# Where the scales of the down tiles, the sums of the next pair and the last group's scale are issued in an encoder block

## The chip, the cores and the metric

The kernel runs on one core of one Trainium2 chip. The metric is the device time of one execution in microseconds (us), the median of the runs. TensorE (PE) does the matmuls, VectorE (DVE) and ScalarE (ACT) work on tiles in SBUF and PSUM, and loads are issued on the queues of SyncE (SP) and GpSimd (POOL).

## The reference

One layer of a hybrid encoder block on 512 positions of width 2048, in float32. It ends with a gated feed-forward part, which is all that the change touches:

```python
h2 = rms_norm(x, g_ffn[l])
up = causal_dwconv(h2 @ w_up[l], conv_w[l], conv_b[l])   # w_up 2048 x 11264, width-3 taps
a, gate = jnp.split(up, 2, axis=-1)
x = x + (a * jax.nn.silu(gate)) @ w_down[l]              # w_down 5632 x 2048
```

## The kernel before

Weights come from HBM as float32 tiles of 128x1024. So that TensorE can run at its f16 rate, each tile is scaled by a factor that suits its largest row sum and split into two f16 halves, high and low, in one tile `whl` (`split16`, L886: ACT writes the high half on L889, DVE the low half on L890). A product then takes three f16 matmuls for each block: high by high, high by low, low by high (`mm3`, L130).

**Units.** The hidden width is cut into 44 pairs of column blocks (a column block of `a` and the matching one of `gate`). The first four pairs are done by `lead`. Each pair j from 4 to 43 is a unit (`up_unit`, L988): it multiplies a 2x2 block matrix by Strassen's scheme (Winograd's form), so it takes seven products instead of eight, T4, B11, T1, T2, B21, B22, T3, in this order, of 24 matmuls each. Their seven weight tiles are made from four loads and sums of them: `s1` (two tiles added by an accumulating POOL DMA), `a22`, `a11`, `a12`, then `s2` and `s4` (DVE adds in place, L948 and L952), and `s3` (again two tiles added by a DMA). After the seventh product DVE combines the PSUM banks into `z`, the taps follow (L827 to L829), and `gated` (L835) makes the hidden tile `m` of the pair on DVE (L838) and its row sums on ACT (L841).

**Down tiles.** Behind each unit from the fifth pair on, two down tiles are multiplied (`down`, L1059): 24 matmuls each of 512 columns into two PSUM tiles named `mx`, which DVE adds to the accumulators (L1078). The last ten down tiles follow the last unit. Four pairs make a group; a group's hidden tiles are scaled together (`m_scale`) and split (`m_split`, tiles `mhl`) while the first unit of the next group runs, piece by piece from the list `later`.

**Scales.** A scale is one number for all partitions. `abs_sums` (L893) lets ACT sum the absolute values of each row of a tile (tile `junk`, sums in `sm`). `scales` (L763) then takes the row maximum (DVE, L770), puts it on the diagonal of a 128x128 tile (ACT, `dg`, L771), multiplies by ones on TensorE so that each partition sees all 128 maxima (L773, into an `mx` tile), and takes maximum, product and reciprocal on DVE (L774 to L776). `period_scales` does this for a unit and its two down tiles at once: six sums, one multiplication of 256 columns.

**Order.** The program is a list `todo` of steps; a unit has seven steps that make weight tiles, and one for each of its down tiles. Ahead of each product or down tile, `take(3)` runs steps until four weight tiles are ready, so that in the steady state the step run at a product is three places further on. At the seventh product of unit j (T3) that is the first step of unit j+1, `start`, which calls `period_scales`; at the first down tile behind unit j it is the second step of unit j+1. Each engine issues its instructions in one fixed order. That order is not the text's: a planner at build time lets an instruction pass earlier ones that are not ready by its own estimate.

**Pools.** Tiles come from pools by tag. `junk`, `su` (the copy of B11's bank, L997), `mhl` and `m` are all of the tag `act` (48 buffers); the PSUM tiles of L773 and of the down tiles are all of the tag `mx` (4 buffers); raw down tiles have 3 buffers (`raw`), the unit's loads 4 (`ur`), the split tiles 3 under each of two tags.

Of the kernel before, what the change touches and what calls it, by code (L numbers as in the profile page):

```python
# [8 lines left out]
F32 = mybir.dt.float32  # L9
# [4 lines left out]
AF = mybir.ActivationFunctionType  # L14
ALU = mybir.AluOpType
PSUM = bass.MemoryType.PSUM

P = 128
# [5 lines left out]
NPAIR_FF = 44  # L24
N_WARM = 12
NGRP = 11
N_LEAD = 4
H = 256
BND = 16000.0
# [18 lines left out]
C_CW = C_CB + 88  # L48
# [4 lines left out]
def block_kernel(ctx: ExitStack, tc: tile.TileContext, xT, wst, cols, bias_t, masks, yT):  # L53
# [17 lines left out]
    def nm(s):  # L71
        cnt[0] += 1
        return f"{s}{cnt[0]}"
# [10 lines left out]
    def sm_t():  # L84
        return smp.tile([P, 8], F32, tag="sm", name=nm("sm"))
# [4 lines left out]
    def mx_t():  # L90
        return ps_mx.tile([P, T], F32, tag="mx", name=nm("mx"))

    V = nc.vector
    A = nc.scalar
# [3 lines left out]
    def c3(ap, n):  # L98
        return ap.rearrange("p (a b) -> p a b", a=n)
# [36 lines left out]
    colt = cst.tile([P, NC], F32, name="colt")  # L136
# [52 lines left out]
    one = cst.tile([P, 1], F32, name="one")  # L189
# [547 lines left out]
    cwp = ctx.enter_context(tc.tile_pool(name="cwp", bufs=3))  # L737
# [25 lines left out]
    def scales(sets, bound):  # L763


        n = len(sets)
        t = sm_t()
        dg = dgp.tile([P, 2, P], BF16, tag="dg", name=nm("dg"))
        for i, r in enumerate(sets):
            V.tensor_reduce(out=t[:, i:i + 1], in_=r, axis=mybir.AxisListType.X, op=ALU.max)  # L770
            A.activation(dg[:, i], ident, AF.Copy, scale=t[:, i:i + 1])  # L771
        psm = c3(mx_t()[:, 0:2 * P], 2)
        PE.matmul(psm[:, 0:n], lhsT=on1b, rhs=dg[:, 0:n], start=True, stop=True)  # L773
        V.tensor_reduce(out=t[:, 2:2 + n], in_=psm[:, 0:n], axis=mybir.AxisListType.X, op=ALU.max)  # L774
        V.tensor_scalar(out=t[:, 4:4 + n], in0=t[:, 2:2 + n], scalar1=1.01 / bound, scalar2=1e-30, op0=ALU.mult, op1=ALU.add)
        V.reciprocal(out=t[:, 6:6 + n], in_=t[:, 4:4 + n])  # L776
        return [(t[:, 4 + i:5 + i], t[:, 6 + i:7 + i]) for i in range(n)]

    def junk_t():
        return actp.tile([P, 1024], F16, tag="act", name=nm("junk"))  # L780

    gs = cst.tile([P, KT], F32, name="gs")
    inv_h = cst.tile([P, 1], F32, name="inv_h")
# [78 lines left out]
    todo, ready, later = [], [], []  # L862
# [16 lines left out]
    def load_sum(t, i, k):  # L879
        nc.sync.dma_start(out=t, in_=wst[i])  # L880
        nc.gpsimd.dma_start(out=t, in_=wst[k], accum_op=ALU.add)
        return t
# [10 lines left out]
    def abs_sums(r, tiles):  # L893
        for k, t in enumerate(tiles):
            A.activation(junk_t(), t, AF.Abs, accum_out=r[:, k:k + 1])  # L895

    units = {}
    DOWNS = [(g, c2) for g in range(NGRP) for c2 in range(8)]
    N_BESIDE = 2 * (NPAIR_FF - N_LEAD - 1)

    def unit_loads(j):
        u = units.setdefault(j, {})
        i = N_MIX + 16 + 4 * (j - N_LEAD)
        u["s1"] = load_sum(ur_t(), i + 2, i + 3)
        u["a22"] = load(ur_t(), i + 3)
        u["a11"] = load(ur_t(), i)
        u["a12"] = load(spare2 if j % 2 else ur_t(), i + 1)

    def down_loads(ds):
        at_end = DOWNS.index(ds[0]) - N_BESIDE  # L910
        new = ur_t if at_end >= 0 and at_end % 4 == 0 else raw_t
        return [load(new(), N_DOWN + 8 * g + c2) for g, c2 in ds]

    def period_scales(j, ds):

        r = sm_t()
        sets = []
        u = units.get(j)
        if u is not None:
            abs_sums(r[:, 0:4], [u[n] for n in ("s1", "a22", "a11", "a12")])  # L920
            sets.append(r[:, 0:4])
        if ds:
            raws = down_loads(ds)
            abs_sums(r[:, 4:8], raws)
            sets.append(r[:, 4:4 + len(ds)])
        sc = scales(sets, BND)
        dt = [(raw, *sc[-1]) for raw in raws] if ds else []
        if u is not None:
            h = cwp.tile([P, 1], F32, tag="uh", name=nm("uh"))
            V.tensor_tensor(out=h, in0=sc[0][0], in1=inv_h, op=ALU.mult)  # L930
            cw = cwp.tile([P, 2, 3], F32, tag="cw", name=nm("cw"))
            A.activation(cw, c3(colt[:, C_CW:C_CW + 3 * 88], 2)[:, :, 3 * j:3 * j + 3], AF.Copy, scale=h)
            u.update(s=sc[0][1], cw=cw, ds=dt)
        return dt

    def plan_unit(j, ds):
        u = units.setdefault(j, {})

        def whl(n):
            ready.append(split16(u[n], u["s"]))  # L940

        def start():
            if "s" not in u:
                period_scales(j, ds)
            whl("a22")

        def s2():
            V.tensor_tensor(out=u["a11"], in0=u["s1"], in1=u["a11"], op=ALU.add)  # L948
            whl("a11")

        def s4():
            V.tensor_tensor(out=u["a12"], in0=u["a11"], in1=u["a12"], op=ALU.add)  # L952
            whl("a12")
            if j + 1 < NPAIR_FF:
                unit_loads(j + 1)

        def s3():
            i = N_MIX + 16 + 4 * (j - N_LEAD)
            u["s3"] = load_sum(raw_t() if j == N_LEAD else spare, i, i + 2)
            whl("s3")  # L960

        todo.extend([start, lambda: whl("a11"), lambda: whl("s1"), s2, lambda: whl("a12"), s4, s3])
        todo.extend([lambda k=k: down_split(u["ds"][k]) for k in range(len(ds))])

    def down_split(d):
        raw, inv, s = d
        ready.append((split16(raw, s), inv))

    def plan_downs(ds):

        st = []

        def one(k):
            if k == 0:
                st.extend(period_scales(None, ds))
            down_split(st[k])
        todo.extend([lambda k=k: one(k) for k in range(len(ds))])

# [45 lines left out]
    def lead():  # L1024
        half = N_LEAD // 2
        n = 0
        for j in range(half):
            u = c3(ur_t(), 2)
            for e in range(2):
                ps = mm_t()  # L1030
                for h in range(2):
                    wh, wl = next_w()
                    for k in range(8):
                        cs = slice(k * P, (k + 1) * P)
                        kt = 8 * h + k
                        mm3(ps, wh[:, cs], wl[:, cs], hh[kt], hl_[kt], kt == 0, kt == KT - 1)
                        if n == 0 and k == 3:
                            finish_r2()
                    if n in (2, 4, 6):
                        t_prep(n // 2 - 1)  # L1040
                    n += 1
                evict_r2(ps, u[:, e])
            lead_taps(j, [u[:, 0], u[:, 1]], (ssa, rmask)[j])
        unit_loads(N_LEAD)
        pss = [mm_t() for _ in range(2 * half)]
        for i in range(8):
            wh, wl = next_w()
            for e, kt in enumerate((i, i + 8)):
                for c in range(2 * half):
                    cs = slice((4 * e + c) * P, (4 * e + c + 1) * P)  # L1050
                    mm3(pss[c], wh[:, cs], wl[:, cs], hh[kt], hl_[kt], i + e == 0, i + e == 8)
            if i in (1, 2, 4, 6, 7):
                t_prep((0, 3, 4, 0, 5, 0, 6, 7)[i])
            if i == 4:
                period_scales(N_LEAD, [])
        us = [evict_r2(ps, actp.tile([P, T], F32, tag="act", name=nm("u"))) for ps in pss]
        later.extend([lambda j=j: lead_taps(half + j, us[2 * j:2 * j + 2]) for j in range(half)])

# [22 lines left out]

    mrp = ctx.enter_context(tc.tile_pool(name="mrp", bufs=2))
    steps = []
    queue = DOWNS
    done = 0
    for j in range(N_LEAD, NPAIR_FF):
        steps.append(j)
        n = 0 if j == N_LEAD else 2
        ds = queue[done:done + n]
        done += n  # L1090
        plan_unit(j, ds)
        steps += ds
    for k in range(done, len(queue), 2):
        plan_downs(queue[k:k + 2])
    steps += queue[done:]

    gate_taps = colt[:, C_CW + 3 * (NPAIR_FF + N_LEAD):C_CW + 3 * 88]
    A.activation(gate_taps, gate_taps, AF.Copy, scale=-1.0)
# [2 lines left out]
    for st in steps:  # L1101
        if isinstance(st, tuple):
            down(*st)
            continue
        up_unit(st)
        if st == N_LEAD:
            m_scale(0)
            for j in range(4):
                m_split(j)
        elif st % 4 == 3:  # L1110
            g = st // 4
            later.append(lambda g=g: (m_scale(g), m_split(4 * g)))
            later.extend([lambda j=j: m_split(j) for j in range(4 * g + 1, 4 * g + 4)])
        if st == NPAIR_FF - 1:
            while later:
                later.pop(0)()


def _level_masks(np):
# [121 lines left out]
```

## Time and profile before

| | us |
|---|---|
| median of 3 runs | 2279.82 |
| lowest and highest | 2278.26, 2281.75 |
| the profiled execution | 2279.07 |
| its span, first to last instruction | 2277.3 |
| PE busy in the span | 2200.5 (97%) |
| DVE busy | 1672.4 (73%) |
| ACT busy | 1336.8 (59%) |
| DMA queue q1, share of 16 engines | 32.4% |

The profiled execution lies 0.75 us under the median. The feed-forward units run from about 1010 to 2199 us of the span, the last ten down tiles with the two of the last unit from 2199 us to the end. A busy share is an average over the span; what a stage waits for is seen in the waits and the timeline of that stage.

### The profile page before, as it was taken

How to read it: one execution, taken by the hardware profiler on the slowest of the kernel's cores; microseconds unless marked ns; L12 is line 12 of the kernel's file. 1: busy time of each engine (PE TensorE's matmuls, PEld its weight loads, DVE VectorE, ACT ScalarE, POOL GpSimd, SP SyncE). 2: the span in 40 equal slices, each digit the busy share in tenths (PEclk: the TensorE clock that was granted, in tenths of full speed). 3: DMA queues.
4: the chain of work that ended last, by engine and by line, in shares of the span. 5: the costliest groups of instructions: out<-in, count | busy, mean ns of one | idle time of the engine just before them, and what ended most of it. 6: DMA issues, size and time to landing. Idle time of an engine off the chain costs nothing.

```text
span 2277.3 us, 34675 instructions
## 1 busy us (share of the span) xinstructions
PE 2200.5 (97%) x13667; PEld 1694.6 (74%) x13667; DVE 1672.4 (73%) x2729; ACT 1336.8 (59%) x2119; POOL 271.3 (12%) x261
## 2 busy tenths in 40 slices
PE   9999999999999999998999999999999999999989
PEld 7888888788888888785667777776776777777654
DVE  7678658857658744787777777787877777778764
ACT  5455445545445424457676767776667776767661
POOL 5223123310001103100000000000000000000001
PEclk9999999999999999999999999999999999999999
DMA  6222222232222333445555565555555666655532
GB/s 211 88 70 75 84 93 65 77 99 84 86 91 93 125 117 101 129 140 131 166 158 164 161 162 162 158 157 153 148 164 158 167 167 167 158 156 160 149 91 83
DMA packets 82755, 294.21 MB, mean 129 GB/s; under 512 B 9568, under 2 KB 10208, under 8 KB 82592
## 3 DMA queue, kind: packets, MB, share of 16 engines
q1 hardware_dynamic: 68112, 240.34, 32.4%
q0 software_dynamic: 14480, 51.65, 12.0%
q8 instruction: 107, 1.75, 0.3%
q14 instruction: 56, 0.46, 0.1%
HBM read 287.76 MB, written 4.19 MB: 128 GB/s over the span
## 4 chain that ended last, share of the span: by engine, by line
PE 49%; DVE 28%; ACT 11%; issue 6%; DMA 6%; POOL 0%; SPq 0%; ACTq 0%; DVEq 0%; POOLq 0%
PE mm L131 12%; PE mm L133 12%; PE mm L132 12%; DVE whl L890 8%; DMA raw<-wst 5%; ACT junk L895 4%; ACT whl L889 4%; DVE vo L1078 3%; PE mx L133 3%; PE mx L131 3%; PE mx L132 3%; DVE vo L828 2%; DVE vo L829 2%; DVE ur L948 1%; ACT dg L771 1%
## 5 line engine op out<-in xcount | busy, mean ns | idle before, releaser
L131 PE MATMUL mm<-th,whl 128*128 128x256 f16 x2240 | 612.5, 273 | 5.9 <-ACT whl L889 5.9
L133 PE MATMUL mm<-th,whl 128*128 128x256 f16 x2240 | 612.3, 273 | 2.6 <-DVE whl L890 2.6
L132 PE MATMUL mm<-tl,whl 128*128 128x256 f16 x2240 | 612.3, 273 | 0.0
L131 PE MATMUL mm<-act,whi 128*128 128x512 f32 x1024 | 406.4, 397 | 0.0
L133 PE MATMUL mm<-act,wlo 128*128 128x512 f32 x1024 | 399.4, 390 | 0.0
L131 PEld LDWEIGHTS <-whl 128*128 128x128 f16 x2948 | 289.1, 98 | 147.9 <-issue 32.0
L132 PE MATMUL mm<-act,whi 128*128 128x512 f32 x1024 | 398.8, 389 | 0.0
L133 PEld LDWEIGHTS <-whl 128*128 128x128 f16 x2948 | 289.2, 98 | 133.7 <-issue 22.5
L132 PEld LDWEIGHTS <-whl 128*128 128x128 f16 x2948 | 289.2, 98 | 108.5 <-issue 0.8
L889 ACT ACTIVATE whl<-ur,sm 128x1024 f16<-128x1024 f32 x206 | 231.1, 1142 | 154.2 <-DVE ur L948 52.1
L119 ACT CAST whi<-raw 128x1024 fp32r<-128x1024 f32 (+1 forms) x161 | 167.7, 1042 | 228.9 <-PE mm L132 183.7
L890 DVE SCALAR_TENSOR_TENSOR whl<-ur,sm,whl 128x1024 f16<-128x1024 f32 x206 | 261.4, 1277 | 41.0 <-ACT whl L889 41.0
L122 DVE TENSOR_TENSOR wlo<-raw,whi 128x1024 fp32r<-128x1024 f32 (+1 forms) x161 | 209.5, 1302 | 91.5 <-ACT whi L119 86.7
L131 PE MATMUL mx<-mhl,whl 128*128 128x512 f16 x708 | 268.5, 379 | 0.0
L132 PE MATMUL mx<-mhl,whl 128*128 128x512 f16 x708 | 268.4, 379 | 0.0
L133 PE MATMUL mx<-mhl,whl 128*128 128x512 f16 x708 | 268.2, 379 | 0.0
L133 PEld LDWEIGHTS mm<-act,wlo 128*128 128x128 f32 x1024 | 192.2, 188 | 41.2
L131 PEld LDWEIGHTS mm<-act,whi 128*128 128x128 f32 x1024 | 192.4, 188 | 38.8 <-issue 0.5
L132 PEld LDWEIGHTS mm<-act,whi 128*128 128x128 f32 x1024 | 192.5, 188 | 38.1 <-issue 0.5
L895 ACT ACTIVATE junk<-ur 128x1024 f16<-128x1024 f32 x146 | 152.1, 1044 | 0.0
L1078 DVE SCALAR_TENSOR_TENSOR vo<-mx,inv,vo 128x512 f32<-128x512 f32 x177 | 130.3, 741 | 25.1 <-PE mx L133 25.1
L890 DVE SCALAR_TENSOR_TENSOR whl<-raw,sm,whl 128x1024 f16<-128x1024 f32 x83 | 106.3, 1283 | 43.1 <-ACT whl L889 42.2
(285 smaller groups left out, 3022.7 us busy)
## 6 DMA issues: line engine op xcount, KB each, us to landing
raw<-wst SPq DMA_DIRECT2D x242, 512.0 KB, 3.5
ur<-wst SPq DMA_DIRECT2D x146, 512.0 KB, 3.5
spare<-wst SPq DMA_DIRECT2D x59, 512.0 KB, 4.8
ur<-wst POOLq DMA_DIRECT2D x40, 512.0 KB, 5.6
spare<-wst POOLq DMA_DIRECT2D x39, 512.0 KB, 8.0
vo<-xT SPq DMA_DIRECT2D x16, 256.0 KB, 5.3
vo<-xT POOLq DMA_DIRECT2D x16, 256.0 KB, 3.1
yT<-vo POOLq DMA_DIRECT2D x13, 256.0 KB, 2.3
```

Of the source, the lines that this page charges most:

```text
L119: A.copy(out=hi[:, c], in_=raw[:, c])
L122: V.tensor_tensor(out=lo[:, c], in0=raw[:, c], in1=hi[:, c].bitcast(F32), op=ALU.subtract)
L131: PE.matmul(ps, lhsT=sh, rhs=mh, start=start, stop=False)
L132: PE.matmul(ps, lhsT=sh, rhs=ml, start=False, stop=False)
L133: PE.matmul(ps, lhsT=sl, rhs=mh, start=False, stop=stop)
L771: A.activation(dg[:, i], ident, AF.Copy, scale=t[:, i:i + 1])
L828: V.scalar_tensor_tensor(out=y[:, 1:], in0=u[:, :T - 1], scalar=cw[:, 1:2], in1=y[:, 1:], op0=ALU.mult, op1=ALU.add)
L829: V.scalar_tensor_tensor(out=y[:, 2:], in0=u[:, :T - 2], scalar=cw[:, 0:1], in1=y[:, 2:], op0=ALU.mult, op1=ALU.add)
L889: A.activation(t[:, 0:1024], x, AF.Copy, scale=s)
L890: V.scalar_tensor_tensor(out=t[:, 1024:], in0=x, scalar=s, in1=t[:, 0:1024], op0=ALU.mult, op1=ALU.subtract)
L895: A.activation(junk_t(), t, AF.Abs, accum_out=r[:, k:k + 1])
L1078: V.scalar_tensor_tensor(out=acc[c][:, ts_], in0=ps[:, ts_], scalar=inv, in1=acc[c][:, ts_], op0=ALU.mult, op1=ALU.add)
```

## The change

`period_scales` is split into three functions. `unit_sums` makes the row sums of chosen tiles of a unit, `unit_scale` makes the unit's scale from the four sums, and `down_scale` makes the scale of a pair of down tiles, with an L773 multiplication of its own (128 columns). They are called from other steps:

- the loads of unit j+1 and the sums of its `s1` and `a22` in the step that splits `a12` of unit j; the sums of its `a11` and `a12` in the step of `s4`; its scale in the step of `s3`, so all ahead of the steps that split the down tiles of unit j
- the loads of unit j+1's down tiles in the last step of unit j (the last down split), and their scale in the second step of unit j+1, behind the split of `a11`
- `m_scale` of the last group, with its four splits, was run right behind the last unit; now the scale and the first split come behind two more down tiles, the other three splits behind a third

```diff
-    def period_scales(j, ds):
+    def unit_sums(j, names):
+        u = units[j]
+        if "r" not in u:
+            u["r"] = sm_t()
+        for n in names:
+            k = ("s1", "a22", "a11", "a12").index(n)
+            abs_sums(u["r"][:, k:k + 1], [u[n]])
+
+    def unit_scale(j):
+        u = units[j]
+        (inv, s), = scales([u["r"][:, 0:4]], BND)
...
+    def down_scale(raws):
         r = sm_t()
...
+        abs_sums(r, raws)
+        (inv, s), = scales([r[:, 0:len(raws)]], BND)
+        return [(raw, inv, s) for raw in raws]
...
-        def start():
-            if "s" not in u:
-                period_scales(j, ds)
-            whl("a22")
+        def p1():
+            whl("a11")
+            if ds:
+                u["ds"] = down_scale(u["raws"])
...
+        def p2():
+            whl("a12")
+            if nxt:
+                unit_loads(j + 1)
+                unit_sums(j + 1, ("s1", "a22"))
+
         def s4():
             V.tensor_tensor(out=u["a12"], in0=u["a11"], in1=u["a12"], op=ALU.add)
             whl("a12")
-            if j + 1 < NPAIR_FF:
-                unit_loads(j + 1)
+            if nxt:
+                unit_sums(j + 1, ("a11", "a12"))
...
             whl("s3")
+            if nxt:
+                unit_scale(j + 1)
...
-        todo.extend([start, lambda: whl("a11"), lambda: whl("s1"), s2, lambda: whl("a12"), s4, s3])
-        todo.extend([lambda k=k: down_split(u["ds"][k]) for k in range(len(ds))])
+        todo.extend([lambda: whl("a22"), p1, lambda: whl("s1"), s2, p2, s4, s3])
+        for k in range(max(len(ds), 1)):
+            def one(k=k):
+                if ds:
+                    down_split(u["ds"][k])
+                if k == max(len(ds), 1) - 1 and nxt:
+                    units[j + 1]["raws"] = down_loads(beside(j + 1))
...
     for st in steps:
         if isinstance(st, tuple):
             down(*st)
+            if st in DOWNS[N_BESIDE - 1:N_BESIDE + 1] and later:
+                later.pop(0)()
+                while later and st == DOWNS[N_BESIDE]:
+                    later.pop(0)()
             continue
...
-        if st == NPAIR_FF - 1:
-            while later:
-                later.pop(0)()
```

## Rows read from the trace of the kernel before

**Rows 1.** Span and granted clock of the core.
```profile
core 0: 2277.3 us, clock 0.996
```

**Rows 2.** Waits of PE in the feed-forward units: us in total, times, longest us.
```profile
PE mx L773 <- ACT dg L771: 46.8, 34, 9.7
PE mm L131 <- ACT whl L889: 5.9, 3, 3.3
```

**Rows 3.** Groups by form, 1130 to 2200 us: busy us, mean ns | idle before us.
```profile
L773 PE MATMUL mx<-dg,on1b 128*128 128x256 bf16 x35 | 9.4, 270 | 32.6 <-ACT dg L771 32.6
```

**Rows 4.** Timeline of PE at four L773 multiplications: start, us, [idle before <- releaser].
```profile
1153.23 0.27 PE L773 MATMUL mx<-dg,on1b 128*128 128x256 bf16 x1 [2.02 <-ACT dg L771]
...
1272.94 0.27 PE L773 MATMUL mx<-dg,on1b 128*128 128x256 bf16 x1 [2.02 <-ACT dg L771]
1273.05 0.27 PE L133 MATMUL mm<-th,whl 128*128 128x256 f16 x1
...
1301.59 0.27 PE L773 MATMUL mx<-dg,on1b 128*128 128x256 bf16 x1 [0.55 <-ACT dg L771]
...
2108.28 0.27 PE L773 MATMUL mx<-dg,on1b 128*128 128x256 bf16 x1 [2.01 <-ACT dg L771]
```

**Rows 5.** Timeline of PE behind the last unit's seventh product.
```profile
2198.83 0.27 PE L133 MATMUL mm<-th,whl 128*128 128x256 f16 x1
...
2208.77 0.27 PE L773 MATMUL mx<-dg,on1b 128*128 128x128 bf16 x1 [9.67 <-ACT dg L771]
2208.83 0.63 PE L131 MATMUL mx<-mhl,whl 128*128 128x512 f16 x1
2209.26 0.63 PE L132 MATMUL mx<-mhl,whl 128*128 128x512 f16 x1
```

**Rows 6.** Timeline of PE from a seventh product over two down tiles to the next unit.
```profile
1243.53 0.27 PE L132 MATMUL mm<-tl,whl 128*128 128x256 f16 x1
1243.64 0.27 PE L133 MATMUL mm<-th,whl 128*128 128x256 f16 x1
1243.75 0.38 PE L131 MATMUL mx<-mhl,whl 128*128 128x512 f16 x1
...
1254.11 0.27 PE L131 MATMUL mm<-th,whl 128*128 128x256 f16 x1
```

**Rows 7.** Timeline of ACT in a unit without group splits.
```profile
1230.24 0.35 ACT L997 COPY su<-mm 128x256 f32<-128x256 f32 x1
1230.49 1.15 ACT L889 ACTIVATE whl<-raw,sm 128x1024 f16<-128x1024 f32 x1
...
1239.20 1.06 ACT L895 ACTIVATE junk<-raw 128x1024 f16<-128x1024 f32 x1 [1.32 <-DMA raw<-wst]
```

**Rows 8.** Timeline of ACT in the next unit, which has the group splits.
```profile
1260.58 1.13 ACT L889 ACTIVATE whl<-raw,sm 128x1024 f16<-128x1024 f32 x1
1262.16 1.34 ACT L856 ACTIVATE mhl<-m,mg 128x512 f16<-128x512 f32 x2 [0.45 <-DVE mg L850]
1263.40 0.35 ACT L997 COPY su<-mm 128x256 f32<-128x256 f32 x1
...
1265.93 1.05 ACT L895 ACTIVATE junk<-ur 128x1024 f16<-128x1024 f32 x1
...
1268.01 1.05 ACT L895 ACTIVATE junk<-ur 128x1024 f16<-128x1024 f32 x1
...
1274.17 1.15 ACT L889 ACTIVATE whl<-ur,sm 128x1024 f16<-128x1024 f32 x1 [1.28 <-DVE uh L930]
```

**Rows 9.** Timeline of DVE around the stretch of rows 6, and behind the last unit.
```profile
1243.46 1.28 DVE L890 SCALAR_TENSOR_TENSOR whl<-ur,sm,whl 128x1024 f16<-128x1024 f32 x1 [1.17 <-ACT whl L889]
...
1252.57 0.68 DVE L838 TENSOR_TENSOR m<-vo,vo 128x512 f32<-128x512 f32 x1
1253.17 0.74 DVE L1078 SCALAR_TENSOR_TENSOR vo<-mx,inv,vo 128x512 f32<-128x512 f32 x1
1253.83 1.21 DVE L948 TENSOR_TENSOR ur<-ur,ur 128x1024 f32<-128x1024 f32 x1
...
2206.59 0.69 DVE L838 TENSOR_TENSOR m<-vo,vo 128x512 f32<-128x512 f32 x1 [0.76 <-ACT vo L837]
```

**Rows 10.** Timeline of ACT behind the last unit.
```profile
2207.31 0.63 ACT L841 ACTIVATE z<-m 128x512 f32<-128x512 f32 x1 [0.76 <-DVE m L838]
2207.85 0.19 ACT L841 ACTIVATION_READ_ACCUMULATOR z<-m 128x1 f32 x1
...
2209.98 2.56 ACT L856 ACTIVATE mhl<-m,mg 128x512 f16<-128x512 f32 x4 [1.25 <-DVE mg L850]
```

**Rows 11.** Timeline of the SP queue, loads for the next unit.
```profile
1255.11 4.77 SPq L876 DMA_DIRECT2D ur<-wst  x2
```

**Rows 12.** Stretches: us, busy us (x instructions) of PE, PEld, DVE, ACT, POOL; PE clock; DMA.
```profile
1054.00:1058.00 4.00, 0.68 (x7) 0.37 (x5) 0.10 (x1) 1.28 (x2) 0.00 (x0) 1.00 0.73 267
1059.77:1063.18 3.41, 3.25 (x16) 2.14 (x15) 1.50 (x4) 3.03 (x8) 0.09 (x1) 0.50 0.71 205
...
2203.24:2213.48 10.24, 4.71 (x12) 1.73 (x12) 6.98 (x15) 5.74 (x11) 0.00 (x0) 0.50 0.12 44
```

More of the change, by code (lines that the diff above doesn't have):

```diff
@@ L912, in down_loads @@
         return [load(new(), N_DOWN + 8 * g + c2) for g, c2 in ds]
-    def period_scales(j, ds):
-        r = sm_t()
[L917 to L934, printed above, removed]
+    def unit_sums(j, names):
[8 more added lines that the diff above has]
+        (inv, s), = scales([u["r"][:, 0:4]], BND)
+        h = cwp.tile([P, 1], F32, tag="uh", name=nm("uh"))
+        V.tensor_tensor(out=h, in0=inv, in1=inv_h, op=ALU.mult)
+        cw = cwp.tile([P, 2, 3], F32, tag="cw", name=nm("cw"))
+        A.activation(cw, c3(colt[:, C_CW:C_CW + 3 * 88], 2)[:, :, 3 * j:3 * j + 3], AF.Copy, scale=h)
+        u.update(s=s, cw=cw)
+    def down_scale(raws):
+        r = sm_t()
+        abs_sums(r, raws)
+        (inv, s), = scales([r[:, 0:len(raws)]], BND)
+        return [(raw, inv, s) for raw in raws]
     def plan_unit(j, ds):
         u = units.setdefault(j, {})
+        nxt = j + 1 < NPAIR_FF
         def whl(n):
             ready.append(split16(u[n], u["s"]))
-        def start():
-            if "s" not in u:
-                period_scales(j, ds)
-            whl("a22")
+        def p1():
+            whl("a11")
+            if ds:
+                u["ds"] = down_scale(u["raws"])
         def s2():
@@ L960, in s3, with beside @@
             whl("s3")
-        todo.extend([start, lambda: whl("a11"), lambda: whl("s1"), s2, lambda: whl("a12"), s4, s3])
-        todo.extend([lambda k=k: down_split(u["ds"][k]) for k in range(len(ds))])
+            if nxt:
[7 more added lines that the diff above has]
+                    units[j + 1]["raws"] = down_loads(beside(j + 1))
+            if ds:
+                todo.append(one)
+            else:
+                todo[-1] = lambda f=todo[-1]: (f(), one())
+    def beside(j):
+        i = 2 * (j - N_LEAD - 1)
+        return DOWNS[i:i + 2] if i >= 0 else []
     def down_split(d):
@@ L974, in one @@
             if k == 0:
-                st.extend(period_scales(None, ds))
+                st.extend(down_scale(down_loads(ds)))
             down_split(st[k])
@@ L1054, in lead @@
             if i == 4:
-                period_scales(N_LEAD, [])
+                unit_sums(N_LEAD, ("s1", "a22", "a11", "a12"))
+                unit_scale(N_LEAD)
         us = [evict_r2(ps, actp.tile([P, T], F32, tag="act", name=nm("u"))) for ps in pss]
@@ L1083, in block_kernel @@
     steps = []
-    queue = DOWNS
-    done = 0
     for j in range(N_LEAD, NPAIR_FF):
+        plan_unit(j, beside(j))
         steps.append(j)
[L1088 to L1095, printed above, removed]
+        steps += beside(j)
+    for k in range(N_BESIDE, len(DOWNS), 2):
+        plan_downs(DOWNS[k:k + 2])
+    steps += DOWNS[N_BESIDE:]
     gate_taps = colt[:, C_CW + 3 * (NPAIR_FF + N_LEAD):C_CW + 3 * 88]
```

## The prediction

> **What bounds the kernel now.** I read the clock first: 0.996 of full over the span [rows 1], that is some 18 to 20 us at half clock in all, so throttling is rare now. Then the waits of PE in the feed-forward units: nearly all is one line, L773 waiting for ACT's `dg`, 46.8 us in 34 waits [rows 2]. PE is otherwise streaming, a matmul of 256 columns every 0.11 us [rows 6], so every microsecond of PE's waits is a microsecond of the kernel, and nothing else is. From 1130 to 2200 us it is 32.6 us at 35 multiplications [rows 3]. The timeline splits this in two kinds. In the unit that also splits a group (every fourth, nine in all, first and last of them shown) the wait is 2.0 us each time, which is 18 us [rows 4]. The other 26 there share 32.6 - 18.1 = 14.5 us, a mean of 0.56 us; the one at 1301.59 with 0.55 is typical [rows 4]. The longest is behind the last unit: 9.67 us for the last group's scale, and then 10.24 us at clock 0.5 in which PE worked 4.71 [rows 5, 12], so another 2.4 us lost.
>
> **Two orders that the rows show.** They decide this case. First, behind the last unit PE stood 9.67 us at L773 although the next down tile was ready: that tile's PSUM tile has the tag `mx` too and comes later in the text [rows 5]. Second, in a unit without group splits ACT copies `su` (L997) at 1230.24, ahead of the split of a raw tile [rows 7]; in the unit with them the raw split at 1260.58 goes first and L997 only at 1263.40, behind two `mhl` [rows 8], though B11, which it copies, was over near 1254.11 + 48 x 0.11 = 1259.4 [rows 6]. `mhl` and `su` share the tag `act`, and those two `mhl` stand earlier in the text. So the planner, which else lets instructions pass each other, begins the tiles of one tag in the order of the text, whether or not a buffer is free. I take this to hold also when one tile is begun by DVE and the other by ACT, which no row shows.
>
> **The change, part by part.**
>
> The down pair's scale. Steps run three places ahead, so the second step of unit j+1 runs at the first down tile behind unit j, and that is behind `gated` of unit j in the text. Its `junk` tiles therefore come behind `m` of unit j (tag `act`), and its L773 comes ahead of that down tile's PSUM tiles (tag `mx`). Before, the step ran at T3, ahead of `gated`. So the down tiles behind unit j now wait for unit j's own hidden tile. From the last matmul of T3 to L838 it is 1252.57 - 1243.64 = 8.9 us with down evictions between [rows 6, 9], 2206.59 - 2198.83 = 7.8 us without [rows 5, 9]; I take 8.9, the stretch within the loop. Then two row sums at 1.04 [rows 8], L841 at 0.7, and 0.9 from its last part to L773 (2207.85 to 2208.77) [rows 5, 10]: 3.7. The down tiles can start 12.6 us behind T3 (11.5 at least). What hides this: the next unit's products, which need none of it. Four of them are 4 x 24 x 0.11 = 10.6 us, and the fifth 2.6; the planner does pass a late L773 with matmuls, as at 1272.94, where it stands inside a product [rows 4]. The weight tiles for them are made in the previous unit's second half, since the unit's scale is now early. So the down tiles move into the next unit, with no idle time by plan. What remains is how late L773 is against the plan: that is also what the 0.56 us is now. I take the same 0.56 at the 30 ordinary units, a sum of 0. Bounds: no wait, -17 us; 2.0 us at each, the nearest row above [rows 4], 1.45 x 30 = +43 us.
>
> The unit's scale in units that split a group. In text order `mx` runs: down tiles behind unit j-1, `m_scale`, scale of unit j+1. The down tiles end 12.6 + 10.4 (1243.75 to 1254.11 [rows 6]) = 23.0 us behind T3 of unit j-1. `m_scale` follows, its first split 1.2 later (2208.77 to 2209.98 [rows 5, 10]): 24.2. On ACT tag `act` then forces: split 0.67, two sums 2.1, split 0.67, `su` 0.25, two sums 2.1 [rows 8]; 0.9 to L773 as above, and 0.3 for a third split that may come between (0 to 0.67): 31.2. From L773 to the next unit's first weight split 1274.17 - 1272.94 = 1.2 [rows 4, 8], high half 1.15, low half 1.28 [rows 8, 9]: 34.9. PE has by then done seven products and two down tiles, 168 x 0.11 + 10.4 + 0.1 = 29.0, and nothing else may start. The wait is 5.9 us where it was 2.0. With 7.8 for 8.9 it is 4.8; with the whole third split and one DVE eviction (0.7) in front, 6.9. Half clock: PE's 3.32 us wait in 1054 to 1058 (busy 0.68 of 4 us) was followed by 3.41 us at 0.5, a loss of 1.7 us [rows 12]; the waits of 2.0 us left no mark in the mean of 0.996 [rows 1]. I take 1.7 for each wait of 5.9 (0 to 2.4). Per unit 5.9 + 1.7 - 2.0 = 5.6, times nine: +50 us (9 x 2.8 = +25 to 9 x 7.3 = +66).
>
> On the clock the Trainium skill ("TensorE: Matmul & The Clock Gate", section "HAM oscillation") says that a kernel whose matmul bursts are parted by waits falls back to half clock at each of them and pays each time anew. By that the 1.7 us recur at all nine; without it the term would be 9 x 3.9 = +35 us and the time 15 us less.
>
> Loads. The unit's loads stand earlier in the text, but SP issues them at 1255.11, just when L948 (1253.83 + 1.21) frees their buffer [rows 9, 11]; the accumulating loads on POOL's queue follow these. No gain, no loss. The raw loads wait for their buffers too; the 1.32 us in which ACT waited for one [rows 7] leaves the unit's chain.
>
> Small parts. One more chain per unit on DVE and PE: two L773 of 128 columns instead of one of 256 (0.06 from 2208.77 to 2208.83 against 0.11 [rows 4, 5]), three short DVE steps of under 0.3 us beside PE's work. Nothing; if DVE were the bound, 39 x 0.6 = 23 us, but it idles 27% of the span. `su` goes later by some 7 us; its reader L1001 needs T2's product and is not waited for until T3 is over.
>
> The last group. The two down tiles of the last unit now precede `m_scale`. The first runs at once (5.2 us). The second stands behind the scale of the pair 80, 81, whose sums come behind the last `m`: 7.8 + 3.7 = 11.5, a wait of 6.3 us instead of 9.67. `m_scale` is then hidden; the next pair's sums stand behind its four splits: L773 of `m_scale` at 16.8, splits from 18.0 to 20.6, sums and L773 at 23.6, while PE is done at 22.1: 1.5 us. With 2.4 for the clock again 10.2 against 12.1: -2 us (-4 to -1).
>
> Sum: 2279.07 (profiled, 0.75 under the median) + 0 + 50 - 2 = 2327 us. Its own range is the sum of the bounds: +4 to +108, 2283 to 2387.
>
> **The rivals.**
>
> 1. Faster. The order of tag `act` binds only tiles begun on the same engine, or only when buffers run out. Then `junk` doesn't wait for `m`, the unit's sums lie in ACT's idle time, no L773 comes late, and the last group's scale is covered by two down tiles (10.4 us against 9.67). It decides at one point: the down pair's sums ahead of L838. Gain 9 x 2.0 + 30 x 0.56 + 12.1 = 47 us: 2232 us. For it: ACT idles over 40% of the span. Against it: L997 was held while ACT had time [rows 8].
>
> 2. No change. The down tiles move, but the ordinary units' waits vanish (-17) and the group units cost only their lower bound (+25), with -4 at the end: 2283 us, within 0.2%. For it: the ordinary L773 then depends on no load. Against it: all three at their lower ends.
>
> 3. Much slower. The next unit's products don't pass the down tiles. PE would wait out 12.6 us at each of 39 units, less the 35 us of now: 39 x 12.6 - 35 = +456 us, 2735 us. Against it: the place of the L773 at 1272.94 [rows 4].
>
> **How the numbers follow.** Forecast 0.74, rivals 0.13, 0.09 and 0.04. Differences under 0.2% (4.6 us) can't be told from no change here. Faster: rival 1 and a scrap of the forecast's lower tail, 0.14; same: rival 2, 0.09; slower 0.77. The range of 2270 to 2385 leaves out rivals 1 and 3 and a little at the upper end.
>
> **What would show it.** Right: down tiles run between T2 and B21 of the next unit; the pair's L773 stands behind L838; nine waits of PE of 5 to 7 us for ACT's weight split (not for `dg`), each followed by clock 0.5; a wait of about 6 us after the first of the last twelve down tiles. Wrong: `junk<-raw` ahead of L838, or T3 followed by down tiles at once as now (rival 1); PE waits at every unit of over 10 us (rival 3). The term that could be most wrong is the ordinary unit's lateness, for which only the plan's accuracy in other places speaks.

## The result, and the profile after

The changed kernel takes 2350.22 us (median of 4 runs, 2348.90 to 2353.41), the kernel before 2280.18 us beside it: a ratio of 1.031, interval 1.0292 to 1.0327. It is slower, as forecast, and 23 us slower than the 2327 us named; the range of 2270 to 2385 holds it. The profiled execution took 2353.41 us with a span of 2351.6, so 74.3 us more than the profiled one of before in both. Line numbers below are those of each run's own kernel: in the changed one L773, L889 and L895 stay where they were, the last steps of a unit's scale are L927 and L929, and the taps L827 to L829.

The core's span and granted clock, which answer to [rows 1]:

```profile
core 0: 2351.6 us, clock 0.980
```

The waits of PE from 1000 us to the end (us in total, times, longest), which answer to [rows 2]:

```profile
PE mx L773 <- ACT dg L771: 45.4, 47, 5.7
PE mm L131 <- ACT whl L889: 44.1, 12, 5.0
PE mm L133 <- DVE whl L890: 11.9, 13, 1.4
```

PE waits at L773 as long as before, and two rows have grown beside it: PE waits for weight tiles. In total PE waits 101.4 us where it waited 55.3, that is 46.1 of the 74.3 us.

The timeline of PE over one unit that also splits a group (start, us, idle before and its releaser), which answers to [rows 4, 6]:

```profile
1252.78 0.27 PE L133 MATMUL mm<-th,whl 128*128 128x256 f16 x1
1252.89 0.27 PE L131 MATMUL mm<-th,whl 128*128 128x256 f16 x1
...
1264.11 0.22 PE L773 MATMUL mx<-dg,on1b 128*128 128x128 bf16 x1 [0.90 <-ACT dg L771]
1264.16 0.38 PE L131 MATMUL mx<-mhl,whl 128*128 128x512 f16 x1
...
1274.52 0.22 PE L773 MATMUL mx<-dg,on1b 128*128 128x128 bf16 x1
1274.57 0.27 PE L131 MATMUL mm<-th,whl 128*128 128x256 f16 x1
...
1284.20 0.22 PE L773 MATMUL mx<-dg,on1b 128*128 128x128 bf16 x1 [1.27 <-ACT dg L771]
...
1288.36 0.39 PE L131 MATMUL mm<-th,whl 128*128 128x256 f16 x1 [3.95 <-ACT whl L889]
...
1289.90 0.39 PE L133 MATMUL mm<-th,whl 128*128 128x256 f16 x1 [0.93 <-DVE whl L890]
```

The seventh product of a unit ends at 1252.78, and the next unit's first product follows at once (in [rows 6] two down tiles stood there). The down tiles come at 1264.16, behind the pair's L773, 93 matmuls into the next unit, that is three short of the end of its fourth product, T2. Behind them come, at 1274.52, L773 of the group, at 1284.20 L773 of the following unit, and then PE stands for that unit's first weight tile. The three waits, 1.27 + 3.95 + 0.93 = 6.15 us, recur nine times, every 127 to 128 us, the last from 2176.51.

The timeline of ACT and DVE in the same unit, which answers to [rows 8, 9]:

```profile
1260.24 0.69 DVE L838 TENSOR_TENSOR m<-vo,vo 128x512 f32<-128x512 f32 x1
```

```profile
1261.59 1.04 ACT L895 ACTIVATE junk<-raw 128x1024 f16<-128x1024 f32 x1
...
1262.63 1.13 ACT L889 ACTIVATE whl<-ur,sm 128x1024 f16<-128x1024 f32 x1
1263.67 0.39 ACT L771 ACTIVATE dg<-ident,sm 128x128 bf16<-128x128 f32 x1
...
1277.48 0.72 ACT L856 ACTIVATE mhl<-m,mg 128x512 f16<-128x512 f32 x1 [1.61 <-DVE mg L850]
1278.11 1.04 ACT L895 ACTIVATE junk<-ur 128x1024 f16<-128x1024 f32 x1
...
1283.75 0.39 ACT L771 ACTIVATE dg<-ident,sm 128x128 bf16<-128x128 f32 x1
...
1287.17 1.13 ACT L889 ACTIVATE whl<-ur,sm 128x1024 f16<-128x1024 f32 x1
```

From the first `mhl` (1277.48) to `dg` (1283.75) ACT has no idle time: splits of the group, `su` (L1022 here) and the four sums of the next unit, all in the order that the prediction wrote down.

Stretches behind the waits (us, busy us of PE, PEld, DVE, ACT, POOL; clock; DMA), which answer to [rows 12]:

```profile
1159.27:1166.10 6.83, 3.71 (x17) 2.37 (x18) 6.37 (x11) 5.37 (x7) 0.00 (x0) 0.50 0.23 77
1285.56:1295.80 10.24, 6.51 (x30) 4.33 (x31) 9.27 (x15) 6.45 (x8) 0.00 (x0) 0.50 0.16 51
1415.27:1422.10 6.83, 5.06 (x23) 3.21 (x24) 6.79 (x9) 4.19 (x5) 0.00 (x0) 0.50 0.22 77
...
2282.26:2289.09 6.83, 5.34 (x14) 1.97 (x14) 3.31 (x7) 3.74 (x6) 0.00 (x0) 0.50 0.12 24
2299.32:2302.73 3.41, 3.36 (x9) 1.24 (x9) 1.92 (x5) 3.38 (x6) 0.00 (x0) 0.50 0.02 5
```

Each of the nine groups of waits is followed by 6.83 or 10.24 us at granted clock 0.5, the lower level (1.2 GHz). Half of what PE worked in them counts as lost: 46.2 us in the nine, so 23.1. PE behind the last unit, which answers to [rows 5]:

```profile
2283.74 0.27 PE L773 MATMUL mx<-dg,on1b 128*128 128x128 bf16 x1 [5.68 <-ACT dg L771]
...
2299.37 0.26 PE L773 MATMUL mx<-dg,on1b 128*128 128x128 bf16 x1 [2.38 <-ACT dg L771]
```

### The profile page after: what moved, and what is told of

Its sections match the earlier page's. It is cut to its first block, busy times and chain, and to the rows that moved or that the text cites. A ratio compares the mean times of both kernels' runs of the same rounds, so it can differ in the third digit from the quotient of the medians.

```text
span 2351.6 us, 34978 instructions
## 1 busy us (share of the span) xinstructions
PE 2229.1 (95%) x13706; PEld 1704.7 (72%) x13706; DVE 1704.5 (72%) x2846; ACT 1331.0 (57%) x2119; POOL 270.9 (12%) x261
## 4 chain that ended last, share of the span: by engine, by line
PE 60%; DVE 22%; ACT 12%; issue 4%; DMA 2%; SPq 0%; POOL 0%; ACTq 0%; POOLq 0%; DVEq 0%
PE mm L133 12%; PE mm L131 12%; PE mm L132 12%; DVE whl L890 7%; PE mx L133 7%; PE mx L131 7%; PE mx L132 7%; ACT whl L889 5%; ACT junk L895 3%; DVE vo L828 2%; DVE vo L829 1%; DVE z L1030 1%; DVE z L1031 1%; ACT z L841 1%; DVE ur L951 1%
## 5 line engine op out<-in xcount | busy, mean ns | idle before, releaser
L131 PE MATMUL mm<-th,whl 128*128 128x256 f16 x2240 | 622.7, 278 | 44.1 <-ACT whl L889 44.1
L133 PE MATMUL mm<-th,whl 128*128 128x256 f16 x2240 | 621.7, 278 | 11.9 <-DVE whl L890 11.9
L132 PE MATMUL mm<-tl,whl 128*128 128x256 f16 x2240 | 622.7, 278 | 0.0
L131 PEld LDWEIGHTS <-whl 128*128 128x128 f16 x2948 | 292.5, 99 | 212.3 <-ACT whl L889 60.0
L133 PEld LDWEIGHTS <-whl 128*128 128x128 f16 x2948 | 292.7, 99 | 130.3 <-DVE whl L890 17.5
L132 PEld LDWEIGHTS <-whl 128*128 128x128 f16 x2948 | 292.9, 99 | 108.9 <-issue 2.3
L889 ACT ACTIVATE whl<-ur,sm 128x1024 f16<-128x1024 f32 x206 | 233.5, 1141 | 141.0 <-PE mm L133 86.3
L889 ACT ACTIVATE whl<-raw,sm 128x1024 f16<-128x1024 f32 x83 | 93.7, 1143 | 174.9 <-PE mx L133 172.2
L895 ACT ACTIVATE junk<-ur 128x1024 f16<-128x1024 f32 x146 | 152.5, 1046 | 4.1 <-DMA ur<-wst 3.7
```

Of the source, the lines that this page charges most:

```text
L131: PE.matmul(ps, lhsT=sh, rhs=mh, start=start, stop=False)
L132: PE.matmul(ps, lhsT=sh, rhs=ml, start=False, stop=False)
L133: PE.matmul(ps, lhsT=sl, rhs=mh, start=False, stop=stop)
L889: A.activation(t[:, 0:1024], x, AF.Copy, scale=s)
```

## The experiments

**Theory** (that of the forecast): the scale of a down pair now stands behind `m` of the unit in tag `act` and ahead of the down tiles in tag `mx`, so the down tiles run late, and in group units the scale of the group and that of the next unit come late behind them. **Rivals**: ACT simply has too much in front of what PE needs, wherever the tags put it; or the new order would be no better without the tags' orders.

**1. Sums out of the tag `act`.**

```diff
+    djp = ctx.enter_context(tc.tile_pool(name="djp", bufs=1))
-        abs_sums(r, raws)
+        abs_sums(r, raws, down_junk_t)     # junk of down tiles from djp
```

> The changed kernel with one edit: the junk tiles of the down tiles' row sums come from a pool of their own, so their order is no longer tied to the hidden tile m. Theory (tiles of one tag are begun in the order of the text, so the down pair's scale waits for m, and the down tiles for that scale): the down tiles run right behind T3 again, the nine waits for a weight split (about 6 us each, with 6.8 to 10.2 us at half clock behind them) are gone, and the wait of 5.7 us behind the first of the last twelve down tiles too; 2260 us, 2240 to 2275, below the kernel before. Rival (the sums of the next pair, now ahead of the down splits, crowd ACT, so that raw loads and down scales come late): the down tiles' place is a symptom, the waits stay, over 2310 us.

Measured 2288.09 us (ratio to before 1.0036, 1.0023 to 1.005). Down tiles are again right behind the seventh product, the nine waits and the one of 5.68 us are gone: 62 of the 70 us. So the tag's order made the down tiles late; here the rival falls. But the forecast of 2260 fell too. Waits of all engines, 1100 to 2200 us:

```profile
ACT junk L899 <- DMA raw<-wst: 70.5, 36, 5.2
PE mx L774 <- ACT dg L772: 46.4, 49, 2.7
```

ACT now waits 70.5 us for raw loads to land. In the same stretch it waited 14.9 us for them in the kernel before, and not once in the changed one.

**2. The pair's scale one step earlier**, ahead of `gated` in the text.

```diff
-            whl("a11")
+            whl("a22")                     # in p1, followed by down_scale
-        todo.extend([lambda: whl("a22"), p1, ...
+        todo.extend([p1, lambda: whl("a11"), ...
```

> The changed kernel with the down pair's scale made in the first step of its unit instead of the second, which is run at T3, ahead of gated. Theory: the same cure by the order of the text alone, in the loop: 2270 us, 2250 to 2285; behind the last unit the wait of 5.7 us after the first down tile stays, since the pair 80, 81 is still scaled behind m. Rival (crowded ACT): over 2310 us, since the same sums stand at nearly the same place.

Measured 2347.43 us (1.0291, 1.0269 to 1.0314). The order was cured, down tiles stand behind the seventh product, and the time stayed: by its number the rival's. The timeline at one of the long waits, of DVE, of SP, and then of all engines:

```profile
1718.08 1.28 DVE L890 SCALAR_TENSOR_TENSOR whl<-raw,sm,whl 128x1024 f16<-128x1024 f32 x1 [0.88 <-ACT whl L889]
```

```profile
1719.39 0.33 SPq L876 DMA_DIRECT2D raw<-wst  x1
```

```profile
1726.73 1.06 ACT L895 ACTIVATE junk<-raw 128x1024 f16<-128x1024 f32 x1 [4.27 <-DMA raw<-wst]
1727.69 0.19 ACT L895 ACTIVATION_READ_ACCUMULATOR junk<-raw 128x1 f32 x1
1727.78 1.13 ACT L889 ACTIVATE whl<-ur,sm 128x1024 f16<-128x1024 f32 x1
...
1728.82 0.39 ACT L771 ACTIVATE dg<-ident,sm 128x128 bf16<-128x128 f32 x1
...
1729.26 0.26 PE L773 MATMUL mx<-dg,on1b 128*128 128x128 bf16 x1 [3.78 <-ACT dg L771]
```

With three raw buffers, a pair's second load can be issued only when the first down tile of the pair before has been split: 1718.08 + 1.28 = 1719.36, issue at 1719.39. It lands 7.3 us later, while ACT waits. A new suspect, the raw buffers, tried in runs 9 to 12.

**3. The last group alone**: the kernel before with only the last group's scale moved.

```diff
+            if st in DOWNS[N_BESIDE - 1:N_BESIDE + 1] and later:
+                later.pop(0)()
...
-        if st == NPAIR_FF - 1:
-            while later:
-                later.pop(0)()
```

> The kernel before with only the last group's scale moved behind two more down tiles. Theory: the second of these waits for the scale of the pair 80, 81, whose sums stand behind m, so about 6 us of the 9.7 us stay and another 1.5 to 2.5 us come later: 2278 us, 2275 to 2281. Rival (two down tiles of 10.4 us cover the chain of 9.7 us): 2268 us.

Measured 2279.72 us (0.9994, 0.9984 to 1.0004): no difference that can be measured. One wait of 9.7 us became one of 5.7 and one of 2.4, and 6.83 us at half clock stayed. As predicted, this part is worth next to nothing.

**4. A PSUM bank for L773**, on the changed kernel; `mx` keeps three.

```diff
+    banks["mx"] = ctx.enter_context(tc.tile_pool(name="ps_my", bufs=3, space=PSUM))
+    ps_sc = ctx.enter_context(tc.tile_pool(name="ps_sc", bufs=1, space=PSUM))
-        psm = c3(mx_t()[:, 0:2 * P], 2)
+        psm = c3(ps_sc.tile([P, T], F32, tag="sc", name=nm("mx"))[:, 0:2 * P], 2)
```

> The changed kernel with a PSUM bank of its own for the scales' multiplications in the feed-forward part (three left for the down tiles), so that their order is no longer tied to the down tiles' PSUM tiles. Theory (both orders are needed for the harm): down tiles run right behind T3 although the pair's scale still stands behind m; the nine waits are gone; 2265 us, 2240 to 2290. If only the tag act mattered: as the changed kernel, about 2350 us. Rival (crowded ACT): over 2310 us.

Measured 2259.37 us (0.9902, 0.9886 to 0.9918): 91 us less than the changed kernel, and faster than the one before. The timeline of PE:

```profile
1239.20 0.27 PE L133 MATMUL mm<-th,whl 128*128 128x256 f16 x1
1239.31 0.38 PE L131 MATMUL mx<-mhl,whl 128*128 128x512 f16 x1
...
1251.59 0.22 PE L775 MATMUL mx<-dg,on1b 128*128 128x128 bf16 x1 [0.23 <-ACT dg L773]
1251.64 0.27 PE L133 MATMUL mm<-th,whl 128*128 128x256 f16 x1
```

The pair's scale is as late as in the changed kernel (12.4 us behind the seventh product, there 11.3), but its L775 stands between matmuls of the next unit and the down tiles no longer wait for it. All of PE's waits for scales between 1100 and 2200 us are 19.6 us in 65 places, none over 0.7. So a late scale costs little by itself; the harm was that the down tiles had to follow it.

**5. The same bank on the kernel before.** The diff is that of run 4.

> The kernel before, with a PSUM bank of its own for L773 and three for the down tiles from the feed-forward part on; nothing of the change. Theory (the order of the tag mx is what makes a late scale cost PE time, in either kernel): the joint L773 no longer holds the down tiles behind it, so the 33 us of its waits from 1130 us on and the 12 us behind the last unit go for the most part: 2245 us (2230 to 2262). Rival (the gain of the run with the bank on the changed kernel came from the separate chains, the bank only lifted a new harm): the joint L773 waits as before, 2270 to 2282 us.

Measured 2269.94 us (0.9944, 0.9925 to 0.9962), which is the rival's 2270, not the theory's 2262 or less. Groups by form, 1130 to 2200 us, which answers to [rows 3]:

```profile
L775 PE MATMUL mx<-dg,on1b 128*128 128x256 bf16 x35 | 9.4, 270 | 29.6 <-ACT dg L773 29.5
```

The 32.6 us of [rows 3] are still 29.6: there the bank changes nothing, and the theory falls. What went is the 9.67 us behind the last unit with its half clock. The reading that fits, though the plan itself was not looked at: the planner puts L773 where it takes `dg` to be ready, and where `dg` is later than that, PE waits in whatever bank.

**6. Bank and own `junk` together** (the diffs of runs 1 and 4).

> The changed kernel with both orders lifted: own bank for L773, own buffer for the row sums of the down tiles. Theory (the order of mx alone turned the late pair's scale into harm, that of act only made it late): nothing is left for the second buffer to gain but the wait behind the last unit, 2257 us (2248 to 2262). Rival (a late down split still costs PE): 2240 us or less.

Measured 2300.66 us (1.0082, 1.006 to 1.0104): worse than with the bank alone, which neither theory had. Waits of all engines, 1100 to 2200 us:

```profile
ACT junk L901 <- DMA raw<-wst: 65.6, 35, 4.5
PE mx L776 <- ACT dg L774: 40.5, 47, 2.5
PE mx L131 <- DVE vo L1110: 19.8, 18, 1.8
```

The waits for raw loads are those of run 1. In run 4 the tag's order held the sums back until the loads had landed. The third row is new: down tiles wait for DVE to empty an `mx` bank. Three banks alone don't bring it, since run 4 has three and no such row, nor does the own `junk` alone (run 1, four banks); it takes both, and why was not tried.

**7. The bank for the group's scale only**, on the changed kernel.

```diff
-    (inv, s), = scales([rms[g]], BND)
+    (inv, s), = scales([rms[g]], BND, own=True)
```

> The changed kernel with the bank of its own for the scale of a group only (m_scale); the pair's and the unit's L773 stay in mx, of three banks. Theory (in a group unit the scale of the group stood behind the down tiles, so its splits and then the sums of the next pair came late): the nine waits of 6.1 us and the half clock behind them, some 9 x 8.8 = 79 us, go, and 2 us of wait at each stay: 2290 us (2275 to 2305). Rival (the nine waits come from ACT's load in these units, wherever L773 of the group stands): over 2325 us.

Measured 2349.88 us (1.0297, 1.0279 to 1.0316): no gain. PE:

```profile
1273.96 0.38 PE L132 MATMUL mx<-mhl,whl 128*128 128x512 f16 x1
1274.18 0.38 PE L133 MATMUL mx<-mhl,whl 128*128 128x512 f16 x1
1274.40 0.22 PE L776 MATMUL mx<-dg,on1b 128*128 128x128 bf16 x1
...
1288.23 0.40 PE L131 MATMUL mm<-th,whl 128*128 128x256 f16 x1 [3.94 <-ACT whl L892]
```

Free to go earlier, and with its `dg` done on ACT by 1265.3 us, the group's L776 still came behind the two down tiles. They stand earlier in the text, and here they went first. So what has to be mended is the lateness of the down tiles, that is the place of the pair's L773; the bank for the group is no cure.

**8. Early scale and bank** (the diffs of runs 2 and 4).

> The run with the pair's scale one step earlier, which was no faster than the changed kernel, with the bank of its own for L773 added. Theory (its 85 us of waits were PE standing at the pair's L773 with matmuls behind it that needed nothing of it): they go, 2262 us (2250 to 2275). Rival (ACT is too crowded ahead of the down splits, so the down tile's weights are late, wherever L773 stands): over 2310 us.

Measured 2350.47 us (1.0312, 1.0275 to 1.035). Waits of all engines, 1100 to 2200 us:

```profile
PE mx L775 <- ACT dg L773: 87.1, 68, 5.5
ACT junk L897 <- DMA raw<-wst: 83.9, 34, 6.0
```

As in run 5 the bank doesn't help where PE comes to the scale before it is there. That the raw loads make it late is tried in run 11.

**9 to 12. A fourth raw buffer.** To make room, tag `act` has 46 or 47 buffers.

```diff
-    actp = ctx.enter_context(tc.tile_pool(name="actp", bufs=48))
+    actp = ctx.enter_context(tc.tile_pool(name="actp", bufs=47))
+    wp4 = ctx.enter_context(tc.tile_pool(name="wp4", bufs=1))
...
-        return [load(new(), N_DOWN + 8 * g + c2) for g, c2 in ds]
+            k = DOWNS.index((g, c2))
+            t = new() if k % 4 < 3 or new is ur_t else wp4.tile([P, 1024], F32, tag="raw4", ...
```

On run 2 (early scale):

> The run with the pair's scale one step earlier, with a fourth buffer for raw down tiles (and 47 buffers of the tag act for 48, to make room). With three, the second raw load of a pair is issued only when the first down tile of the pair before is split, and ACT waited 70 us for raw loads between 1100 and 2200 us where it waited none in the changed kernel. Theory (PE stands at the pair's L773 because its sums wait for that load, which the plan takes to be there sooner): ACT's waits for raw loads fall under 10 us, those of PE at L773 from 85 us to some 30 to 40 (0.5 each at two per unit), and the time is 2285 us (2260 to 2300). Rival (ACT has too much ahead of the down splits; the load is not what binds): over 2320 us.

Measured 2269.04 us (0.9955, 0.994 to 0.997), 78 us less than run 2. Waits as above:

```profile
PE mx L774 <- ACT dg L772: 25.4, 46, 5.7
ACT junk L896 <- DMA ur<-wst: 16.1, 9, 2.8
```

The row for raw loads is gone, and PE's waits at the scales fell from 74.0 us in this stretch to 25.4. That settles run 2: the load, not ACT's own work.

On run 1 (own `junk`):

> The run with a buffer of its own for the row sums of the down tiles, with a fourth raw buffer (and 46 buffers of the tag act). Its 70 us of ACT's waits for raw loads stood against the order it had cured. Theory (as for the run with the early scale): the waits of 2 to 2.7 us at L774 go and about 0.5 stays at each: 2260 us (2245 to 2275). Rival: 2285 us or more, as without the buffer.

Measured 2252.21 us (0.9881, 0.9866 to 0.9896), 36 us less than run 1 and the fastest of all. On run 8 (early scale and bank):

> Early scale and own bank for L773 (2350 us), with the fourth raw buffer. Theory: with the loads there in time the bank does what it did in the changed kernel: 2258 us (2245 to 2272). Rival (the early scale crowds ACT): over 2310 us.

Measured 2256.29 us (0.9902, 0.9886 to 0.9919). On the kernel before:

> The kernel before with the fourth raw buffer (47 buffers of the tag act) and nothing of the change. Theory (the buffer is needed only by the early scale of the changed order; here the 2.0 us at L773 in the nine group units come from ACT's splits and sums, and the 0.56 us at the others are how late ACT is against the plan anyway): 2276 us (2268 to 2282). Rival (the buffer is what gained in the three runs with it, whatever the order): 2260 us or less.

Measured 2264.19 us (0.9935, 0.9918 to 0.9952), between the two theories. Groups by form, 1130 to 2200 us, which answers to [rows 3]:

```profile
L774 PE MATMUL mx<-dg,on1b 128*128 128x256 bf16 x35 | 9.5, 271 | 19.3 <-ACT dg L772 18.3
```

32.6 us became 18.3 + 1.0, and 18.3 is nearly what the nine waits of 2.0 in group units make. So the 2.0 us do come from ACT's work, as the theory had it, but the 0.56 us at the other units were waits for raw loads. The buffer alone is worth 16 us. Beside it the changed order with its `junk` freed takes another 12 (2264 to 2252); not freed, and with three buffers, it costs 70. The changed order with the fourth buffer and nothing else was not run.

Where those 12 us lie is seen from the profiled executions. All start the units between 1010 and 1011 us and have the same twelve down tiles behind the last unit:

| | start of the last matmul of the last unit, us | from there to the end of the span, us |
|---|---|---|
| before | 2198.83 | 78.5 |
| run 5, bank on before | 2200.32 | 67.3 |
| run 4, bank on changed | 2188.45 | 67.3 |
| run 12, fourth buffer on before | 2183.64 | 78.2 |
| run 10, own `junk` and fourth buffer on changed | 2181.81 | 68.3 |

In the units the changed order (run 10) is 2 us ahead of the old one that has the buffer too (run 12); the other 10 are the stretch behind the last unit, which the bank shortens for the old order too. From runs 5 and 12 together an estimate for the kernel before with buffer and bank, which was not run, is about 2253 us, as fast as run 10. So no run shows that the units need the new order.

## Why the prediction came out as it did

The main forecast was right in its mechanism: down tiles run inside the next unit, waits for weight splits in nine units (1.27 of each 6.15 us is still for `dg`), half clock behind each, and the two waits at the end. Its sum was 26 us short against the profiled execution (+74.3 where it had +48):

| term | predicted | measured | from |
|---|---|---|---|
| nine group units | +50 (25 to 66) | +60 | 9 x 6.15 + 23.1 - 18.1 |
| ordinary units | 0 (-17 to 43) | +7 | L773 from 1130 to 2200 us, 32.8 - 9 x 1.27 = 21.4, less 14.5 |
| last group | -2 (-4 to -1) | 0 | 5.68 + 2.38 + 4.35 less 9.67 + 2.36 |
| first units, 1010 to 1130 us | none | +2 | PE's waits there, 15.3 less 13.0 |

About 5 us of the 74.3 stay unplaced; the 39 multiplications more, 0.05 us each (1264.11 to 1264.16), may be 2 of them.

**The down pair's scale.** Predicted 12.6 us from the seventh product to the down tiles (11.5 at least), measured 1264.16 - 1252.78 = 11.4. The choice between 8.9 and 7.8 for the way to L838 was the wrong one: with the down tiles moved away, their evictions no longer stand ahead of `m`, and it took 1260.24 - 1252.78 = 7.5. From L838 to L773 it was 3.87, predicted 3.7. The next unit's products hid all of this but the 0.90 us before L773, as forecast.

**The unit's scale in group units.** Counted from the seventh product: end of the down tiles 21.7 (predicted 23.0), first `mhl` 24.7 (24.2), L773 31.4 (31.2), low half 1289.90 - 1252.78 = 37.1 (34.9; its terms add up to 34.8). The step that was short is the one from L773 to the first split: 1.2 was taken from a unit of before, and it took 2.97 here (1284.20 to 1287.17), since DVE's steps of the scale now lie among the group's low halves (L857) and the `z` steps, and ACT's split behind a tap. The same step behind the group's L773 took 2.96 for 1.2 (1274.52 to 1277.48); the early end of the down tiles hid that. PE was later too, 30.0 for 29.0, and in the 7.1 us from there to 37.1 it still did L773 and two matmuls at half clock, so its waits came to 6.15 for 5.9.

**Half clock.** The term most mis-sized: 1.7 us for each wait, measured 23.1 / 9 = 2.6, above even the bound of 2.4 (8 of the 10 us that the group units' term was short). The row it came from was a wait of 3.3 us with 3.41 us at half clock behind it [rows 12]; behind 6.15 us in 7.3 (1282.65 to 1289.90) it was 6.83 or 10.24. The trace of before has another such stretch 27 us earlier, among waits of 1.52, 0.38, 1.93 and 0.62 us between 1029 and 1035 us, which the prediction passed over:

```profile
1032.46:1039.29 6.83, 5.20 (x24) 3.48 (x25) 6.66 (x11) 5.67 (x7) 0.00 (x0) 0.50 0.25 77
```

Half of its 5.20 us is 2.6, the value measured now. By the section "HAM oscillation" of the Trainium skill's page "TensorE: Matmul & The Clock Gate" a kernel whose matmul bursts are parted by such waits pays the loss anew at each; the trace agrees for the waits of 6.15 us, nine of nine.

**The ordinary units.** The value 0 was nearly right for a wrong reason. The prediction read the 0.56 us as lateness against the plan, and one wait of 0.55 as typical; the trace of before has waits from under 0.3 to 1.72 us there, and run 12 shows that they were waits for raw loads. Those do vanish with the change, as its step on loads said, and are replaced: at 1262.63 a weight split of 1.13 us stands on ACT between the second sum and `dg`, and PE waits 0.90 (up to 0.90 at the others, and once 1.38).

**The last group.** The wait for the pair's scale was 5.68 us (predicted 6.3), the one for the next pair's 2.38 (1.5), and the half clock behind the two cost 4.35 (2.4), so the gain of 2 us did not come. Run 3 says the same of the part by itself.

**Loads.** "No gain, no loss" for the raw loads holds for the changed kernel. What the prediction missed is that the order it called harmful also hides the lack of a fourth raw buffer: where runs 1 and 2 lift it, ACT waits some 70 us for raw loads, in run 2 for one that takes 7.3 us.

**The two orders.** Runs 1 and 4 bear both out, each by lifting one: without the `act` order the down tiles are back behind the seventh product, without the `mx` order a late scale holds up no down tile. The assumption that no row showed, that the order also holds where one tile is begun by DVE and the other by ACT, can hold in the planner's order only: in run 1, freed from the tag, the pair's second sum starts at 1302.27 and `m` at 1315.15. On the chip nothing ties the two, and in the changed kernel the first `junk` of the pair starts 0.48 us ahead of L838 (1259.76). By the letter that is the sign which the prediction named for rival 1; but the second sum stands behind L838 (1261.59), and the down tiles were late.

**The rivals.** Rival 1's point was the right one to name, but not its price: with the sums freed the time was 2288, not 2232, until the loads came in time too (2252). Its 30 x 0.56 us needed the buffer, and with the changed orders about 0.3 to 0.5 us at many of the scales' multiplications stayed even then or with the bank (runs 4 and 9 to 11). Only the old order with the buffer (run 12) has next to none beside the nine of 2.0 us. Rival 3 was as unlikely as thought: no unit waited for more than 6.2 us.

## What to carry to other kernels

Where a planner begins the tiles of a pool tag in text order, a tag shared by short scale tiles and long products is a queue: before moving a step in the text, list which tiles of its tags it now stands ahead of and behind, and give the short chain a tag of its own if it may be late. A step that is freed to run earlier needs its loads earlier as well, so look at what releases the buffer of the load. And a scale that comes late but with other work placed in front of it cost little here (run 4), while one that comes later than the work placed behind it made TensorE wait in whatever bank (runs 5 and 8). Before crediting a new order with a gain, give the old order the same buffers: here that took more than half of the gain away (run 12).

## What the runs showed of the hardware

The same kind of load, 512 KB, has a median of 3.5 us from issue to landing over the changed kernel's span, but the two raw loads of the stretch of run 2 took 7.3 and 8.5 us, with other loads on SP's and POOL's queues around them. The cause of the difference was not tried apart.

The clock doesn't answer to the length of one wait alone. The wait of 2.0 us in group units left no mark in the kernel before. In run 5 the same wait was followed by 3.41 us at half clock in three of nine units. The stretch behind the first of them there, columns as above:

```profile
1153.04:1156.45 3.41, 3.41 (x16) 2.02 (x14) 1.39 (x7) 2.84 (x4) 0.00 (x0) 0.50 0.58 114
```

At about 1.7 us each that is some 5 us in this execution, part of what run 5 fell short of its theory. The bank need not be the cause: run 3, whose text is that of the kernel before up to the last unit, has the same waits of 2.02 us with 3.41 us at half clock behind two of the nine (L773 at 1271.27 and 1748.77), and run 12 behind one (1151.68). What decides between them is open.
